# Some split weights start 64 bytes later in their tiles, and the last rotation of each attention unit stands earlier on VectorE

## The chip, the cores and the metric

The kernel runs on one core of one Trainium2 chip. The metric is the device time of one execution in microseconds, as the median of several runs; lower is better. The core's engines are TensorE (PE in the profile; its weight loads are shown apart as PEld), VectorE (DVE), ScalarE (ACT), GpSimd (POOL) and SyncE (SP, which issues most of the DMAs). Each engine works through its own list of instructions in order, and the lists meet at semaphores.

## The reference

The input is 256 tokens of width 1024 in float32. The trunk has two layers, each followed by an MLP with a squared ReLU, and a last RMS norm:

```python
for layer in range(2):
    xn = rms_norm(x, norm_mix[layer])
    if layer % 2 == 0:
        x = x + even_mixer(xn, ...)   # neighbourhood attention and latent attention, 8 heads each
    else:
        x = x + odd_mixer(xn, ...)    # three groups of dilated windows, 16 heads, rope on q and k
    x = x + jnp.square(jax.nn.relu(rms_norm(x, norm_mlp[layer]) @ w1)) @ w2   # 1024 -> 4096 -> 1024
return rms_norm(x, norm_final)
```

In the odd mixer, `hcat = xn @ w_in` gives q, k and v for 3 groups and 16 heads of 64; q and k are rotated by `apply_rope`, and the three groups' outputs are combined by their softmax denominators.

## The kernel before

**Split weights.** All big products are made in pieces of float32 that TensorE takes as `float32r`. Every weight chunk is loaded from HBM as a tile `raw` of 128 partitions x 2048 float32. ScalarE writes `whi`, a rounded copy of it (`split`, L201), and VectorE writes `wlo`, the rest `raw - whi` (L202), each in four pieces of 512 columns. The activations are split in the same way, into the two halves of one tile `pair`: for each of the 8 slices k of the width, 256 tokens of the high part and then 256 of the low part, so that both together are 512 columns that lie side by side. A product is the sum of high x high, high x low and low x high.

**What TensorE streams and what it holds.** A matmul streams one operand (the moving one) past another that a LDWEIGHTS has put into the array (the stationary one, 128 columns here). The next matmul's LDWEIGHTS runs while the current matmul streams. Four kinds of matmul matter here:

- MLP, first product (`up`, in `mlp`): L391 streams 512 columns of `pair` past `whi` of w1, and L394 streams the 256 high columns of `pair` past `wlo`. Per layer there are 16 steps j with 16 of each, 512 of each in all.
- MLP, second product (`down_tokens`, through `mm3`, L205 to L207): 512 columns of `whi` or `wlo` of w2 stream past the hidden activations `hh` or `hl`.
- Odd layer, q and k (`qk_steps`): L911 streams 512 columns of `pair` past `whi` of `w_oqk`, L914 the 256 high columns past `wlo`; 8 of each for each of 48 products (8 units of two heads, three weight chunks, two halves).
- Odd layer, values (`value_steps`, through `mm3`): 512 columns of `whi` or `wlo` of `w_ov` stream past 128 tokens of `pair`; 96 of each of the three products.

**Where the tiles lie.** `whi` and `wlo` come from a pool with three buffers each. In the program as it is allocated, `pair` starts at byte 26944 of each partition, 64 bytes past a multiple of 128. All buffers of `whi` (121216, 129408, 137600), of `wlo`, and of `hh` and `hl` start at multiples of 128, and so does each matmul's slice of them. The slices of `pair` all start 64 bytes past one.

**What sets the order.** PE, ACT and DVE work in the order that a scheduler gives: it goes by the order in which the code issues the steps and by a priority. `tc.high_priority(NORM_PRIO)` lifts the steps under it ahead of others that are issued earlier, above all ahead of the splits of weights that are only needed later. In the odd layer, `ODD_PLAN` says which unit's q and k and which values are made beside which unit's attention. `qk_steps` makes three products for a unit, in the order b = 0, 2, 1: the q of group 0, the k of groups 1 and 2, and the q of groups 1 and 2. After each, `rope` rotates the product: the halves of each head are swapped into `sw` (by DMA for b = 0 and 2, by ScalarE at L931 and L932 for b = 1), VectorE multiplies by the cosines (L934) and by the sines (L935), and adds the two (L937 with a split for b = 0, L944 in two halves into `k12` for b = 2, L940 into `q12` for b = 1). The sum of the two products' halves before it (L920, L922) is under the high priority; `rope` is not. A unit's scores begin with the matmuls at L214, on the q of group 0, and go on at L979, which read `q12` and `k12`.

Of the kernel before, what the change touches and what calls it, by code (L numbers as in the profile page):

```python
# [17 lines left out]
F32R = mybir.dt.float32r  # L18
# [5 lines left out]
P = 128  # L24
# [10 lines left out]
WCH = 2048  # L35
# [3 lines left out]
SPLIT_AHEAD = 2  # L39
WPARTS = 4  # L40
NORM_PRIO = 300

QK_ORDER = (0, 2, 1)

# [24 lines left out]
def trunk(ctx, tc, a, out):  # L69
# [6 lines left out]
    wsp = ctx.enter_context(tc.tile_pool(name="wsp", bufs=WBUFS))  # L76
# [54 lines left out]
    specs = []  # L131

    def plan(name, n):
        for j in range(a[name].shape[0]):
            specs.append((a[name][j], n))

    def plan_mlp(layer):
        for j in (0, 1):
            specs.append((a["w1"][layer, j], WCH))
        for j in range(2, 16):  # L140
            specs.append((a["w1"][layer, j], WCH))
            specs.append((a["w2"][layer, j - 2], WCH))
        for j in (14, 15):
            specs.append((a["w2"][layer, j], WCH))

    CV = 416 + 512
    plan("w_cv", 2 * CV)
# [5 lines left out]
    plan("w_oe", 2 * D)  # L153
    plan_mlp(0)
    for kind, *at in odd_weights():
        specs.append((a[kind][tuple(at)], WCH))
    plan("w_oo", 2 * D)
    plan_mlp(1)

    parts = {}  # L160
    state = {"loaded": 0, "split": 0, "used": 0}

    def load_weight(edges=None, earlier=lambda i: None):
        j = state["loaded"]
        src, n = specs[j]
        raw = wraw.tile([P, WCH], F32, tag="raw", name="raw")
        edges = edges or (0, n)
        for i, c in enumerate(slice(*e) for e in zip(edges, edges[1:])):
            earlier(i)
            nc.sync.dma_start(raw[:, c], src[:, c])  # L170
        parts[j] = [raw, None, None]
        state["loaded"] = j + 1

    def cut(j, i, n):
        w = specs[j][1] // n
        return slice(i * w, (i + 1) * w)

    def split_piece(eng=None):
        j, i = divmod(state["split"], WPARTS)
        if i == 0:  # L180
            parts[j][1:] = (wsp.tile([P, WCH], F32R, tag=n, name=n) for n in ("whi", "wlo"))
        raw, hi, lo = (z[:, cut(j, i, WPARTS)] for z in parts[j])
        state["split"] += 1
        return split(hi, lo, raw, eng)
# [120 lines left out]
    def hand_over(accs, last, n):  # L305

        xT, s = pair_tile(), sum_tile()
        for b in range(4):
            last[b]()
            with tc.high_priority(NORM_PRIO):  # L310
                join(b, accs[b], n, xT)
        return xT, s

    def hand_over_tokens(accs, last, n, scale):
# [4 lines left out]
        def leave(h, t):  # L319
            last(h, t)  # L320
            acc, sc = accs[2 * t + h], column(scale, t)
            with tc.high_priority(NORM_PRIO):
                y = ys[h, t] = scratch([512], "y")
# [3 lines left out]
        def turn(h):  # L327
            with tc.high_priority(NORM_PRIO):
                for b in range(2):
# [187 lines left out]
    def even(ep):  # L517
# [75 lines left out]
        with tc.manual_schedule(engines={ENG.PE, ENG.Activation, ENG.DVE}):  # L593
            def views(j, c0, c1):
                if parts[j][1] is None:
                    parts[j][1:] = (wsp.tile([P, WCH], F32R, tag=n, name=n) for n in ("whi", "wlo"))
                return [z[:, c0:c1] for z in parts[j]]

            for k in range(KT):
                upper, lower = prepare(k, 0, xT)  # L600
                upper()
                if k < 4:
                    c0 = k % 2 * CV
                    wc, wv = views(k // 2, c0, c0 + 416), views(k // 2, c0 + 416, c0 + CV)
                else:
                    wc, wv = views(2, (k - 4) * 416, (k - 3) * 416), None
                if k == 0:

                    nc.vector.tensor_copy(wc[1], wc[0])
                    lower()  # L610
                    nc.vector.tensor_tensor(wc[2], wc[0], wc[1].bitcast(F32), op=ALU.subtract)
                else:
                    lower()
                    split(wc[1], wc[2], wc[0])
                if wv:
                    split(wv[1], wv[2], wv[0])

                if k in (3, 5, 6, 7):
                    squares.pop(0)()
                for w, ps_, n in ((wc, pc, 416), (wv, pv, 512)):  # L620
                    if w is not None:
                        for passes in ((0,), (1,), (2,)) if k == 0 else (range(3),):
                            for t in range(NT):
                                product(ps_[t], n, w, k, t, passes)
            state["split"] = 3 * WPARTS
            for i in range(2 * WPARTS):
                split_piece()
            wv = [z.rearrange("p (k n) -> p k n", k=4) for z in parts[3]]
            for t in range(NT):
                for k in range(4, KT):  # L630
                    product(pv[t], 512, [z[:, k - 4] for z in wv], k, t)
                    if (t, k) == (0, 5):
                        r = rstd(s)
            rs = work.tile([P, 2, NT], F32, tag="rs", name="rs", bufs=1)
            for i, n in enumerate((256, 128)):
                nc.vector.tensor_scalar(rs[:, i, :], r, n ** -0.5, None, ALU.mult)
            dg = [diagonal(r, t) for t in range(NT)]
            turn_c = [c_tail(t, pc[t]) for t in range(NT)]
            state["used"] = 4
            for j in range(4):  # L640
                del parts[j]
            for t in range(NT):
                v_out(t, pv[t])
# [176 lines left out]
        at = -5  # L820
# [11 lines left out]
    def odd(op, xT, s):  # L832
# [22 lines left out]

        def value_steps(b, c, prio=NORM_PRIO, tag="acc"):

# [39 lines left out]
        def qk_steps(d, js=QK_ORDER):  # L897


            hold = {}  # L900

            def gemm(b, f, half):
                if f == 0 and half == 0:
                    hold["w"], hold["q"] = weight(), op.tile([P, 2, T], F32, tag="qk32", name="qk32", bufs=2)
                if half == 0:
                    hold["p"] = bank("acc")
                (wh, wl), pq, q32 = hold["w"], hold["p"], hold["q"]

                cut_of = lambda k: slice((f * KT + k) * P, (f * KT + k + 1) * P)
                for k in (range(0, 6), range(6, KT))[half]:  # L910
                    nc.tensor.matmul(two(pq), wh[:, cut_of(k)], xp[:, k], start=k == 0, stop=False)  # L911
                if half == 1:
                    for k in range(KT):
                        nc.tensor.matmul(pq[:, 0:T], wl[:, cut_of(k)], xh[:, k, :], start=False, stop=k == KT - 1)  # L914
                if half == 1:
                    with tc.high_priority(NORM_PRIO):
                        if f == 0:
                            side = scratch([T], "side")
                            nc.scalar.copy(side, pq[:, T:2 * T])
                            nc.vector.tensor_tensor(q32[:, f], pq[:, 0:T], side, op=ALU.add)  # L920
                        else:
                            nc.vector.tensor_reduce(q32[:, f], pq.rearrange("p (h n) -> p n h", h=2), axis=mybir.AxisListType.X, op=ALU.add)  # L922
                if f == 1 and half == 1:
                    rope(b, q32.rearrange("p f n -> p (f n)"))

            def rope(b, pq):

                sw, r1 = op.tile([P, 512], F32, tag="swap", name="sw", bufs=2), scratch([2, T], "r1")
                change = nc.scalar.copy if b == 1 else nc.sync.dma_start
                for r in range(0, P, 64):  # L930
                    change(sw[r:r + 32], pq[r + 32:r + 64])  # L931
                    change(sw[r + 32:r + 64], pq[r:r + 32])  # L932
                sw = sw.rearrange("p (f n) -> p f n", f=2)
                nc.vector.tensor_tensor(r1, pq.rearrange("p (f n) -> p f n", f=2), cosT.unsqueeze(1).broadcast_to([P, 2, T]), op=ALU.mult)  # L934
                nc.vector.tensor_tensor(sw, sw, sinT.unsqueeze(1).broadcast_to([P, 2, T]), op=ALU.mult)  # L935
                if b == 0:
                    nc.vector.tensor_tensor(r1, r1, sw, op=ALU.add)  # L937
                    split(d["q0h"], d["q0l"], r1)
                elif b == 1:
                    nc.vector.tensor_tensor(d["q12"], r1, sw, op=ALU.add)  # L940
                else:
                    for r in (0, 64):
                        cut = lambda z: z[r:r + 64].rearrange("p j (c n) -> p j c n", n=64)
                        nc.vector.tensor_tensor(d["k12"][r:r + 64, :, :, r:r + 64], cut(r1), cut(sw), op=ALU.add)  # L944

            return [lambda v=(b, f, h): gemm(*v) for b in js for f in range(2) for h in range(2)]
# [223 lines left out]
```

## Time and profile before

| | |
|---|---|
| time, median of 3 runs | 742.25 us (741.9 to 743.02) |
| the profiled execution's own time | 742.68 us |
| its span, from the first to the last instruction | 740.9 us |
| busy: PE, PEld, DVE, ACT, POOL | 732.5, 628.5, 538.6, 471.4, 8.4 us |
| HBM read | 127.16 MB |

The even layer takes the first 113 us of the span or so, the first MLP goes to about 290 us, the odd layer to about 553 us, and the second MLP to the end. The profile's durations of matmuls are modelled at their ends, so a row of it says more by where the next row starts: a row "start us, us, engine line ... xN" of the timeline merges N equal matmuls, and the difference of two rows' starts, divided by the count, is the spacing of the matmuls.

### The profile page before, as it was taken

How to read it: one execution, taken by the hardware profiler on the slowest of the kernel's cores; microseconds unless marked ns; L12 is line 12 of the kernel's file. 1: busy time of each engine (PE TensorE's matmuls, PEld its weight loads, DVE VectorE, ACT ScalarE, POOL GpSimd, SP SyncE). 2: the span in 40 equal slices, each digit the busy share in tenths (PEclk: the TensorE clock that was granted, in tenths of full speed). 3: DMA queues.
4: the chain of work that ended last, by engine and by line, in shares of the span. 5: the costliest groups of instructions: out<-in, count | busy, mean ns of one | idle time of the engine just before them, and what ended most of it. 6: DMA issues, size and time to landing. Idle time of an engine off the chain costs nothing.

```text
span 740.9 us, 11984 instructions
## 1 busy us (share of the span) xinstructions
PE 732.5 (99%) x4539; PEld 628.5 (85%) x4539; DVE 538.6 (73%) x1100; ACT 471.4 (64%) x1020; POOL 8.4 (1%) x20
## 2 busy tenths in 40 slices
PE   9999999999999999999999999999999999999996
PEld 6988998888888887888888888888898888888885
DVE  6878859766665666689968886899559765665674
ACT  7788967554455456468877668687857455455441
POOL 0100000000000001000000000000000000000000
PEclk9999999999999999999999999999999999999999
DMA  8773335565555554655664545455546555545501
GB/s 291 313 263 108 115 114 177 175 218 174 197 197 178 202 188 155 232 160 171 208 220 147 221 145 182 139 192 173 188 152 220 178 175 197 197 171 189 206 4 57
DMA packets 24585, 133.17 MB, mean 180 GB/s; under 512 B 3664, under 2 KB 4816, under 8 KB 10192
## 3 DMA queue, kind: packets, MB, share of 16 engines
q1 hardware_dynamic: 24384, 132.28, 52.0%
q8 instruction: 35, 0.57, 0.3%
q14 instruction: 22, 0.18, 0.1%
q10 hardware_dynamic: 144, 0.13, 0.1%
HBM read 127.16 MB, written 1.05 MB: 173 GB/s over the span
## 4 chain that ended last, share of the span: by engine, by line
PE 94%; DMA 1%; DVE 1%; issue 1%; ACT 1%; SPq 1%; POOLq 0%; POOL 0%
PE w L391 16%; PE acc L205 13%; PE acc L207 13%; PE acc L206 13%; PE acc L911 11%; PE w L394 8%; PE acc L914 5%; PE acc L558 2%; PE w L214 1%; PE w L999 1%; PE w L205 1%; PE w L768 1%; PE w L207 1%; PE w L206 1%; PE w L979 1%
## 5 line engine op out<-in xcount | busy, mean ns | idle before, releaser
L202 DVE TENSOR_TENSOR wlo<-raw,whi 128x512 fp32r<-128x512 f32 (+2 forms) x471 | 303.0, 679 | 68.2 <-ACT whi L201 67.6
L201 ACT CAST whi<-raw 128x512 fp32r<-128x512 f32 (+2 forms) x471 | 261.9, 614 | 140.5 <-PE acc L207 57.0
L391 PE MATMUL w<-pair,whi 128*128 128x512 f32 x512 | 125.0, 395 | 0.0
L391 PEld LDWEIGHTS w<-pair,whi 128*128 128x128 f32 x512 | 95.2, 187 | 22.9 <-DVE pair L242 0.6
L911 PE MATMUL acc<-pair,whi 128*128 128x512 f32 x384 | 101.6, 401 | 0.0
L205 PE MATMUL acc<-whi,hh 128*128 128x512 f32 x250 | 97.9, 392 | 0.0
L207 PE MATMUL acc<-whi,hl 128*128 128x512 f32 x250 | 97.7, 391 | 0.0
L206 PE MATMUL acc<-wlo,hh 128*128 128x512 f32 x250 | 97.6, 390 | 0.0
L911 PEld LDWEIGHTS acc<-pair,whi 128*128 128x128 f32 x384 | 67.7, 188 | 12.4 <-issue 0.2
L398 DVE TENSOR_TENSOR u<-w,side 128x256 f32<-128x256 f32 x64 | 26.9, 421 | 57.2 <-ACT side L397 57.1
L394 PEld LDWEIGHTS w<-pair,wlo 128*128 128x128 f32 x512 | 63.4, 188 | 2.9
L394 PE MATMUL w<-pair,wlo 128*128 128x256 f32 x512 | 63.9, 277 | 0.0
L201 ACT CAST hh<-hsq 128x512 fp32r<-128x512 f32 x32 | 19.9, 622 | 56.4 <-DVE hsq L400 56.4
L207 PEld LDWEIGHTS acc<-whi,hl 128*128 128x128 f32 x250 | 47.0, 188 | 9.7
L914 PEld LDWEIGHTS acc<-pair,wlo 128*128 128x128 f32 x384 | 51.2, 188 | 4.4
L205 PEld LDWEIGHTS acc<-whi,hh 128*128 128x128 f32 x250 | 47.0, 188 | 8.7
L206 PEld LDWEIGHTS acc<-wlo,hh 128*128 128x128 f32 x250 | 46.9, 188 | 8.8
L914 PE MATMUL acc<-pair,wlo 128*128 128x256 f32 x384 | 51.9, 278 | 0.0
L205 PE MATMUL acc<-whi,pair 128*128 128x512 f32 x80 | 32.3, 403 | 0.0
L207 PE MATMUL acc<-whi,pair 128*128 128x512 f32 x80 | 31.5, 393 | 0.0
L206 PE MATMUL acc<-wlo,pair 128*128 128x512 f32 x80 | 31.2, 390 | 0.0
L990 ACT ACTIVATE pp<-sn,dmn 128x384 f32<-128x384 f32 x32 | 19.7, 614 | 9.8 <-DVE dmn L988 8.9
(220 smaller groups left out, 1102.4 us busy)
## 6 DMA issues: line engine op xcount, KB each, us to landing
raw<-in_w SPq DMA_DIRECT2D x64, 1024.0 KB, 4.8
raw<-in_w_oqk SPq DMA_DIRECT2D x24, 1024.0 KB, 4.9
raw<-in_w_ov SPq DMA_DIRECT2D x12, 1024.0 KB, 5.0
raw<-in_w_qk SPq DMA_DIRECT2D x4, 1024.0 KB, 8.6
raw<-in_w_oe SPq DMA_DIRECT2D x4, 1024.0 KB, 5.3
sw<-qk SPq DMA_DIRECT2D x64, 64.0 KB, 2.0
raw<-in_w_oo SPq DMA_DIRECT2D x4, 1024.0 KB, 5.3
bias<-in_rpb SPq DMA_DIRECT2D x8, 256.0 KB, 4.6
```

The costliest lines, as they stand in the source:

```text
L201: a = nc.scalar.copy(hi, src).ins
L202: return a, (eng or nc.vector).tensor_tensor(lo, src, hi.bitcast(F32), op=ALU.subtract).ins
L205: nc.tensor.matmul(o, sh, mh, start=first, stop=False)
L206: nc.tensor.matmul(o, sh, ml, start=False, stop=False)
L207: nc.tensor.matmul(o, sl, mh, start=False, stop=last)
L391: nc.tensor.matmul(two(pu[f]), w[0][:, cut_of(k, f)], xT[2][:, k], start=k == 0, stop=False)
L394: nc.tensor.matmul(pu[f][:, 0:T], w[1][:, cut_of(k, f)], xT[0][:, k, :], start=False, stop=k == KT - 1)
L398: nc.vector.tensor_tensor(u[:, f], pu[f][:, 0:T], side[:, f], op=ALU.add)
L558: nc.tensor.matmul(o[:, 0:n], xs[i], (w[1], w[1], w[2])[i], start=(k, i) == (0, 0), stop=(k, i) == (KT - 1, 2))
L911: nc.tensor.matmul(two(pq), wh[:, cut_of(k)], xp[:, k], start=k == 0, stop=False)
L914: nc.tensor.matmul(pq[:, 0:T], wl[:, cut_of(k)], xh[:, k, :], start=False, stop=k == KT - 1)
L990: nc.scalar.activation(pp, sn, AF.Exp, bias=mn, scale=-1.0, accum_out=z)
```

## The change

There are two edits. Between them they leave the arithmetic as it is.

**The offset.** Every `whi` and `wlo` tile becomes 32 columns (128 bytes) wider, and the 2048 columns used start either at its beginning or 16 columns (64 bytes) later, by a table that goes by the weight:

```diff
+LINE = 16
+SHIFTS = {"w1": (LINE, 0), "w_oqk": (LINE, 0), "w_ov": (LINE, LINE), "w_v": (LINE, LINE)}
...
-            specs.append((a[name][j], n))
+            specs.append((a[name][j], n, SHIFTS.get(name, (0, 0))))
...
+    def split_tiles(j):
+        return [wsp.tile([P, WCH + 2 * LINE], F32R, tag=n, name=n)[:, o:o + WCH] for n, o in zip(("whi", "wlo"), specs[j][2])]
...
-            parts[j][1:] = (wsp.tile([P, WCH], F32R, tag=n, name=n) for n in ("whi", "wlo"))
+            parts[j][1:] = split_tiles(j)
```

For w1 and `w_oqk` only `whi` is moved, for `w_ov` and `w_v` (a chunk of the even layer's values) both parts; w2 and the rest stay. Tiles that are allocated behind these buffers move by 768 bytes, a multiple of 128. The buffers of `whi` now start at 121216, 129536 and 137856. With "0" for a start at a multiple of 128 bytes and "64" for 64 bytes past one, the streamed slice and the slice that the next LDWEIGHTS reads during it are:

| matmuls in PE's order, columns | count | streamed, before and now | loaded beside it, before and now |
|---|---|---|---|
| L391 followed by L391, 512 | 480 | 64, 64 | 0, 64 |
| L391 followed by L394, 512 | 32 | 64, 64 | 0, 0 |
| L394 followed by L394, 256 | 480 | 64, 64 | 0, 0 |
| L911 followed by L911, 512 | 324 | 64, 64 | 0, 64 |
| L911 followed by L914, 512 | 48 | 64, 64 | 0, 0 |
| L914 followed by L911, 256 | 32 | 64, 64 | 0, 64 |
| L914 followed by L914, 256 | 336 | 64, 64 | 0, 0 |
| L205 to L207 on `w_ov`, followed by their like, 512 | 274 | 0, 64 | 64, 64 |
| L205 to L207 on w2, followed by their like, 512 | 717 | 0, 0 | 0, 0 |
| L207 on w2 followed by L391, 512 | 24 | 0, 0 | 0, 64 |

Where something else stands between two of them, such as a transpose, they are in no row of the table.

**The rotation.** The call of `rope` for b = 1, the last of a unit's three, comes under the high priority:

```diff
                 if f == 1 and half == 1:
-                    rope(b, q32.rearrange("p f n -> p (f n)"))
+
+                    with tc.high_priority(NORM_PRIO if b == QK_ORDER[-1] else 0):
+                        rope(b, q32.rearrange("p f n -> p (f n)"))
```

Of the engines' orders only VectorE's changes by this, at four places: the rotations of units 0, 2, 5 and 6. PE, ACT, POOL and SP have the same instructions in the same order as before. Line numbers of the changed kernel are 7 higher than before around `split` and `mlp`, and 9 higher from `rope` on.

Unit 5, on VectorE, before (`q_5092` is the unit's `q12`, `k_1_3256` its `k12`, `r` the product with the cosines, `qk` the sum before the rotation; `qk_5315` belongs to the next unit):

```order
L935 TENSOR_TENSOR sw<-sw,sinT 128x512
L922 TENSOR_REDUCE qk_5240<-acc 128x256
L944 TENSOR_TENSOR k_1_3256<-r_5219,sw 64x8x64 x2
L934 TENSOR_TENSOR r_5292<-qk_5240,cosT 128x512
L202 TENSOR_TENSOR wlo<-raw,whi 128x512 x2
L920 TENSOR_TENSOR qk_5315<-acc,side 128x256
L935 TENSOR_TENSOR sw<-sw,sinT 128x512
L202 TENSOR_TENSOR wlo<-raw,whi 128x512
L940 TENSOR_TENSOR q_5092<-r_5292,sw 128x512
L922 TENSOR_REDUCE qk_5315<-acc 128x256
```

And the same stretch of VectorE now:

```order
L944 TENSOR_TENSOR sw<-sw,sinT 128x512
L929 TENSOR_REDUCE qk_5240<-acc 128x256
L953 TENSOR_TENSOR k_1_3256<-r_5219,sw 64x8x64
L943 TENSOR_TENSOR r_5292<-qk_5240,cosT 128x512
L953 TENSOR_TENSOR k_1_3256<-r_5219,sw 64x8x64
L209 TENSOR_TENSOR wlo<-raw,whi 128x512 x2
L944 TENSOR_TENSOR sw<-sw,sinT 128x512
L927 TENSOR_TENSOR qk_5315<-acc,side 128x256
L949 TENSOR_TENSOR q_5092<-r_5292,sw 128x512
L209 TENSOR_TENSOR wlo<-raw,whi 128x512
```

The addition into `q12` moves ahead of one split of a weight piece, which now stands right behind it; the second half of `k12` trades places with the product by the cosines, and both halves still stand ahead of `q12`.

Unit 0, on VectorE, before (`q_3260` is its `q12`, `k_0_3254` its `k12`):

```order
L935 TENSOR_TENSOR sw<-sw,sinT 128x512
L934 TENSOR_TENSOR r_3623<-qk_3583,cosT 128x512
L944 TENSOR_TENSOR k_0_3254<-r_3562,sw 64x8x64 x2
L920 TENSOR_TENSOR qk_3646<-acc,side 128x256
L935 TENSOR_TENSOR sw<-sw,sinT 128x512
L202 TENSOR_TENSOR wlo<-raw,whi 128x512
L940 TENSOR_TENSOR q_3260<-r_3623,sw 128x512
L922 TENSOR_REDUCE qk_3646<-acc 128x256
```

And now:

```order
L943 TENSOR_TENSOR r_3623<-qk_3583,cosT 128x512
L944 TENSOR_TENSOR sw<-sw,sinT 128x512
L209 TENSOR_TENSOR wlo<-raw,whi 128x512
L953 TENSOR_TENSOR k_0_3254<-r_3562,sw 64x8x64
L944 TENSOR_TENSOR sw<-sw,sinT 128x512
L927 TENSOR_TENSOR qk_3646<-acc,side 128x256
L949 TENSOR_TENSOR q_3260<-r_3623,sw 128x512
L953 TENSOR_TENSOR k_0_3254<-r_3562,sw 64x8x64
```

Here the split moves ahead of `k12`, and half of `k12` now stands behind `q12`; L979 reads both, so what it needs is complete after the same number of VectorE instructions as before.

More of the change, by code (lines that the diff above doesn't have):

```diff
@@ L134, in plan @@
         for j in range(a[name].shape[0]):
-            specs.append((a[name][j], n))
+            specs.append((a[name][j], n, SHIFTS.get(name, (0, 0))))
     def plan_mlp(layer):
         for j in (0, 1):
-            specs.append((a["w1"][layer, j], WCH))
+            specs.append((a["w1"][layer, j], WCH, SHIFTS["w1"]))
         for j in range(2, 16):
-            specs.append((a["w1"][layer, j], WCH))
-            specs.append((a["w2"][layer, j - 2], WCH))
+            specs.append((a["w1"][layer, j], WCH, SHIFTS["w1"]))
+            specs.append((a["w2"][layer, j - 2], WCH, (0, 0)))
         for j in (14, 15):
-            specs.append((a["w2"][layer, j], WCH))
+            specs.append((a["w2"][layer, j], WCH, (0, 0)))
     CV = 416 + 512
@@ L155, in trunk @@
     for kind, *at in odd_weights():
-        specs.append((a[kind][tuple(at)], WCH))
+        specs.append((a[kind][tuple(at)], WCH, SHIFTS[kind]))
     plan("w_oo", 2 * D)
@@ L164, in load_weight @@
         j = state["loaded"]
-        src, n = specs[j]
+        src, n, _ = specs[j]
         raw = wraw.tile([P, WCH], F32, tag="raw", name="raw")
@@ L595, in views @@
                 if parts[j][1] is None:
-                    parts[j][1:] = (wsp.tile([P, WCH], F32R, tag=n, name=n) for n in ("whi", "wlo"))
+                    parts[j][1:] = split_tiles(j)
                 return [z[:, c0:c1] for z in parts[j]]
```

## The prediction

> **What bounds the kernel now.** I read the page's busy times first, then the chain that ended last, then TensorE's waits.
>
> ```profile
> span 740.9 us, 11984 instructions
> PE 732.5 (99%) x4539; PEld 628.5 (85%) x4539; DVE 538.6 (73%) x1100; ACT 471.4 (64%) x1020; POOL 8.4 (1%) x20
> PE 94%; DMA 1%; DVE 1%; issue 1%; ACT 1%; SPq 1%; POOLq 0%; POOL 0%
> ```
>
> ```profile
> PE acc L117 <- DVE warm L112: 1.2, 1, 1.2
> PE w L979 <- DVE q L940: 0.7, 1, 0.7
> PE acc L205 <- DVE obl L202: 0.2, 1, 0.2
> ```
>
> The second fence is all that PE waited for: 1.2 us at the start, and inside the program 0.7 and 0.2 us. So two things alone can shorten the kernel: that L979 doesn't wait, worth 0.7 us, or that matmuls follow each other more closely. The groups by form say which matmuls there are:
>
> ```profile
> L391 PE MATMUL w<-pair,whi 128*128 128x512 f32 x512 | 125.0, 395 | 0.0
> L911 PE MATMUL acc<-pair,whi 128*128 128x512 f32 x384 | 101.6, 401 | 0.0
> L206 PE MATMUL acc<-wlo,hh 128*128 128x512 f32 x250 | 97.6, 390 | 0.0
> L394 PE MATMUL w<-pair,wlo 128*128 128x256 f32 x512 | 63.9, 277 | 0.0
> ```
>
> Their busy times overlap, so the spacing is read from the starts in the timeline. One step of the first MLP, L391 and L394, then the second product's L205 to L207:
>
> ```profile
> 158.51 3.89 PE L391 MATMUL w<-pair,whi 128*128 128x512 f32 x16
> 162.25 1.99 PE L394 MATMUL w<-pair,wlo 128*128 128x256 f32 x16
> 164.07 0.39 PE L205 MATMUL acc<-whi,hh 128*128 128x512 f32 x1
> ...
> 165.22 0.39 PE L207 MATMUL acc<-whi,hl 128*128 128x512 f32 x1
> ...
> 169.53 0.39 PE L391 MATMUL w<-pair,whi 128*128 128x512 f32 x1
> ```
>
> 16 L391 take 162.25 - 158.51 = 3.74 us, 233.8 ns each. Between 165.22 and 169.53 stand 19 matmuls of w2, 226.8 ns each. Both kinds stream 512 columns past 128, and neither waits. They differ in where the operands lie: for L391 the streamed slice starts 64 bytes past a multiple of 128 and the loaded one at a multiple (I write 64/0); for w2 both start at multiples (0/0). The 16 L394, 64/0 with 256 columns, take 113.8 ns each. Three more spacings, of the odd layer's q and k (L911, 64/0), of its values (0/64), and of the last products of the kernel (256 columns, 0/0):
>
> ```profile
> 400.37 2.02 PE L911 MATMUL acc<-pair,whi 128*128 128x512 f32 x8
> 402.23 1.07 PE L914 MATMUL acc<-pair,wlo 128*128 128x256 f32 x8
> ```
>
> ```profile
> 295.00 0.39 PE L205 MATMUL acc<-whi,pair 128*128 128x512 f32 x1
> ...
> 302.78 0.39 PE L206 MATMUL w<-wlo,pair 128*128 128x512 f32 x1
> ```
>
> ```profile
> 730.21 0.28 PE L205 MATMUL w<-whi,hh 128*128 128x256 f32 x1
> ...
> 734.40 0.28 PE L207 MATMUL w<-whi,hl 128*128 128x256 f32 x1
> ```
>
> L911: 1.86 us for 8, 232.5 ns each. Values: 34 spacings in 7.78 us, 228.8 ns. The last ones: 35 spacings in 4.19 us, 119.7 ns. With 512 columns equal halves are the closest (226.8, against 228.8 and 233.8); with 256 columns it is the other way about, 119.7 with equal halves and 113.8 with unequal ones.
>
> **The offset, part by part.** It brings the 512-column matmuls on w1, `w_oqk` and `w_ov` to 64/64, which no row of before shows with this kind of weight load. The bounds are 226.8 ns, if what counts is that both operands lie in equal halves, and 235.5 ns, if each operand past its multiple costs by itself (the streamed one 233.8 - 226.8 = 7.0, the loaded one 228.8 - 226.8 = 2.0). I take 226.8: the 256-column rows exclude a plain price for the streamed operand's place, since there 64/0 is the closer one, by 5.9 ns.
>
> - w1: 480 pairs L391-L391 x (233.8 - 226.8) = 3.4 us. The 32 pairs that lead to L394 stay 64/0, and so do L394's own, which are at their closer spacing already.
> - `w_oqk`: a block of eight L911 takes 1.86 us; then 7 x 226.8 + 233.8 (the last, before L914, stays 64/0) = 1.82 us, 0.04 less, x 48 blocks = 1.9 us. Against it, 32 L914 that stand before an L911 become 64/64: 32 x 5.9 = 0.2 us. Net 1.7 us.
> - `w_ov`: 274 pairs x 2.0 = 0.5 us.
> - `w_v`: 24 matmuls by the same 2 ns, under 0.1 us; the 24 L207 before an L391 become 0/64, 24 x 2.0 = 0.05 us the other way. Together nothing.
>
> The sum is 5.6 us. All of it lies on the path, since PE is busy without a gap there. What must keep up is hidden work with room:
>
> ```profile
> L202 DVE TENSOR_TENSOR wlo<-raw,whi 128x512 fp32r<-128x512 f32 x456 | 295.5, 684 | 66.6 <-ACT whi L201 66.0
> L202 DVE TENSOR_TENSOR hl<-hsq,hh 128x512 fp32r<-128x512 f32 x32 | 22.1, 691 | 2.4
> L922 DVE TENSOR_REDUCE qk<-acc 128x256 f32<-128x512 f32 x24 | 16.5, 687 | 8.7 <-PE acc L914 8.5
> 290.00:553.00 263.00, 262.18 (x1830) 227.33 (x1829) 210.65 (x426) 193.34 (x407) 2.60 (x3) 1.00 0.54 180
> ```
>
> The second row reads a tile at 64 and one at 0, and takes 691 ns where the first, all at 0, takes 684: 7 ns is my bound for what the moved `whi` costs VectorE, on an engine that is idle for 52 us of the odd layer's 263 (the last row, of the busy times by stretch: PE, PEld, DVE, ACT, POOL, the clock, the DMA share). There it waits for PE (third row), so it starts sooner when PE comes sooner. If that cover were gone, PE would wait at L979 or at the transposes, and up to the odd layer's share, 2.2 us, would be given back.
>
> The Trainium skill, SBUF — State Buffer, section "SBUF: two separate sides", says that on the engines' side only the port that VectorE and GpSimd share is contended and that PE never waits for anyone; and, also of the Trainium skill, TensorE: Matmul & The Clock Gate, section "Step-by-step: what each phase is for", gives TensorE two independent read ports, for the streamed operand and for the weights. By these the offset's 5.6 us would be nothing. The trace disagrees as far as it goes: equal shapes, none waiting, at 226.8 and 233.8 ns.
>
> **The rotation, step by step.** The 0.7 us are in unit 5:
>
> ```profile
> 472.12 0.69 DVE L935 TENSOR_TENSOR sw<-sw,sinT 128x512 f32<-128x512 f32 x1 [1.39 <-DMA sw<-qk]
> ...
> 476.87 0.68 DVE L935 TENSOR_TENSOR sw<-sw,sinT 128x512 f32<-128x512 f32 x1
> 477.46 0.68 DVE L202 TENSOR_TENSOR wlo<-raw,whi 128x512 fp32r<-128x512 f32 x1
> 478.07 0.68 DVE L940 TENSOR_TENSOR q<-r,sw 128x512 f32<-128x512 f32 x1
> ```
>
> ```profile
> 477.86 0.28 PE L214 MATMUL w<-q0h,q0l 64*128 64x256 f32 x2
> ...
> 478.81 1.09 PE L979 MATMUL w<-k,q 128*64 128x128 f32 x16 [0.66 <-DVE q L940]
> ```
>
> The split at 477.46 stands ahead of L940, and now behind it: L940 starts 0.61 us sooner and L979 with it, at about 478.2 instead of 478.81. Since PE also arrives here a little sooner (three blocks of eight L911 stand between 472 and 477, 0.1 us), I count 0.5 us. VectorE's chain from 472.12 on has no gap, so nothing else of it moves; the split that is put off is one of many made ahead. In the other three units PE didn't wait for L940, and nothing is won. The swaps for b = 1 are ScalarE's, whose order stays, and no DMA is moved.
>
> **Sum.** 5.6 + 0.5 = 6.1 us off the profiled execution's own 742.68 us (its span of 740.9 and 1.8 around it) is 736.6; this execution lay 0.4 above the median, so off 742.25: 736.2 us.
>
> **The rivals.**
>
> - *Both places cost by themselves.* Then 64/64 is 235.5 ns: L391 480 x 1.7 = 0.8, L911 324 x 2 = 0.6, `w_ov` 274 x 6.7 = 1.8, 3.2 us in all, less 0.5 for the rotation: 742.25 + 2.7 = 745.0. For it speaks that 64/0 and 0/64 are the same distance apart and cost 7.0 and 2.0 ns, so it isn't the distance alone; and these rows, where L911 at 64 stands before a transpose whose weights lie at 64:
>
> ```profile
> 426.60 1.55 PE L911 MATMUL acc<-pair,whi 128*128 128x512 f32 x6
> 427.99 0.27 PE L999 MATMUL w<-ident,pp 128*128 128x128 f32 x1
> ```
>
> 1.39 us for six is 231.7 ns, no closer; but only one of the six is 64/64, and before another kind of load. Against it speak the 256-column rows. It decides if L391's spacing comes out above 233.8. Chance 0.06.
> - *The place doesn't matter to TensorE*, and the 7 ns come from elsewhere, such as the kind of output or the order of the loads. Only the rotation is left: 741.75. The two spacings that reverse between 512 and 256 columns speak against it. Chance 0.07. The two rules of the Trainium skill named above would give this time.
> - *What counts is the place within 256 bytes.* The wider tiles put every other buffer 128 bytes off, so that only a third of the pairs would be equal: 5.6 / 3 + 0.5 = 2.4 us, 739.9; w2's own pairs would be unequal in two of three too, at a price between 0 and 7.0 ns x 717 x 2/3 = 3.3 us, so up to 743.2. No row of before tells 128 from 256, since all these buffers lie 8192 bytes apart. Chance 0.08, half of it above 740.8.
> - *The gain is partly given back* by waits in the odd layer, as costed above: 736.2 + 2.2 = 738.4. Chance 0.09.
>
> **How the numbers follow.** My forecast, 736.2, has 0.70. Its own range is 734.8 to 737.6: a spacing read over 19 matmuls is good to 0.5 ns, 0.5 us over some 1100 pairs, and the runs of before lay 1.1 us apart. The range that should hold the time 8 times in 10 reaches over the waits given back and to the case of 256 bytes: 734.2 to 740.0. A difference of 0.2%, 1.5 us, is about what a measurement of this kernel can tell from no change: faster means below 740.8, slower above 743.7. Faster: 0.70 for the forecast, 0.09 for the gain partly given back and 0.04 for half of the 256 bytes, 0.83. Same: 0.07 and the other 0.04, 0.11. Slower: 0.06.
>
> **What would show it right or wrong.** In the changed profile, 16 L391 in 3.64 us instead of 3.74 and blocks of eight L911 in 1.82 show the offset's terms; w2's matmuls should stay at 226.8 and L394's at 113.8. L979 should no longer be among PE's waits with more than 0.2 us. L391 at 233 with w2 unchanged refutes equal halves; L391 that differs from step to step by buffer, in turns of three, shows the 256 bytes; new PE waits in the odd layer show the gain given back. A time above 740.8 makes the prediction wrong.

## The result, and the profile after

The changed kernel takes 746.4 us (median of 6 runs, 746.02 to 746.67) against 742.28 us of the kernel before beside it: a ratio of 1.0054, 95% interval 1.0041 to 1.0067. It is slower by 4 us, where 6 us less had been forecast.

The page of the changed kernel, its span and busy times, and then all that TensorE waits for (in each row: what it waited with and the line, the releaser, us in total, times, longest):

```profile
span 744.5 us, 11981 instructions
...
PE 736.5 (99%) x4539; PEld 631.6 (85%) x4539; DVE 540.1 (73%) x1100; ACT 471.4 (63%) x1020; POOL 8.4 (1%) x20
```

```profile
PE acc L121 <- DVE warm L116: 1.2, 1, 1.2
PE acc L565 <- ACT whi L208: 0.5, 1, 0.5
PE acc L212 <- DVE obl L209: 0.2, 1, 0.2
```

The span is 3.6 us longer (740.9 before) and PE's busy time 4.0 us longer, with the same 4539 matmuls. No wait explains it: the 0.7 us at L979 (now L988) are gone, and one of 0.5 us has come at the start of the program. So the matmuls themselves follow each other less closely. Three groups of before that the prediction did not quote:

```profile
L205 PE MATMUL acc<-whi,hh 128*128 128x512 f32 x250 | 97.9, 392 | 0.0
L207 PE MATMUL acc<-whi,hl 128*128 128x512 f32 x250 | 97.7, 391 | 0.0
L914 PE MATMUL acc<-pair,wlo 128*128 128x256 f32 x384 | 51.9, 278 | 0.0
```

And the groups of the changed kernel (L398 was L391, L918 was L911, L212 to L214 were L205 to L207, L401 was L394, L921 was L914):

```profile
L398 PE MATMUL w<-pair,whi 128*128 128x512 f32 x512 | 124.1, 394 | 0.0
L918 PE MATMUL acc<-pair,whi 128*128 128x512 f32 x384 | 101.1, 400 | 0.0
L212 PE MATMUL acc<-whi,hh 128*128 128x512 f32 x250 | 99.1, 397 | 0.0
L214 PE MATMUL acc<-whi,hl 128*128 128x512 f32 x250 | 98.3, 393 | 0.0
L213 PE MATMUL acc<-wlo,hh 128*128 128x512 f32 x250 | 98.2, 393 | 0.0
L401 PE MATMUL w<-pair,wlo 128*128 128x256 f32 x512 | 65.4, 280 | 0.0
L921 PE MATMUL acc<-pair,wlo 128*128 128x256 f32 x384 | 52.8, 280 | 0.0
```

The two groups that the change was to shorten did get shorter, by 0.9 and 0.5 us. The groups that were to stay grew: w2's three by 1.2, 0.6 and 0.6 us, L401 by 1.5, L921 by 0.9. Since the rows overlap, I also summed the distances from each matmul's start to the next one's, group by group, over the whole trace. The differences to before are, in us:

| | after | forecast |
|---|---|---|
| L398, streams `pair`, loads `whi` of w1 | -0.95 | -3.4 |
| L918, the same in the odd layer | -0.54 | -1.9 |
| values of the odd layer, 512 columns | +0.38 | -0.5 |
| w2, three lines | +2.74 | 0 |
| L401, 256 columns past `wlo` of w1 | +1.49 | 0 |
| L921, the same in the odd layer | +0.97 | +0.2 |
| L221, with the wait before L988 | -0.74 | -0.5 |
| all others, above all the first 14 us with the new wait | +0.33 | 0 |
| sum | +3.68 | -6.1 |

The sum is the longer span to within 0.1 us. Two steps of the first MLP in the timeline of the changed kernel show the manner of it:

```profile
147.90 3.80 PE L398 MATMUL w<-pair,whi 128*128 128x512 f32 x16
151.54 2.05 PE L401 MATMUL w<-pair,wlo 128*128 128x256 f32 x16
153.43 0.39 PE L212 MATMUL acc<-whi,hh 128*128 128x512 f32 x1
...
159.03 3.88 PE L398 MATMUL w<-pair,whi 128*128 128x512 f32 x16
162.74 2.04 PE L401 MATMUL w<-pair,wlo 128*128 128x256 f32 x16
164.62 0.39 PE L212 MATMUL acc<-whi,hh 128*128 128x512 f32 x1
...
170.12 1.56 PE L398 MATMUL w<-pair,whi 128*128 128x512 f32 x6
```

The first step's 16 L398 take 3.64 us (227.5 ns each, the forecast's spacing), the second's 3.71 (231.9). L401 takes 1.89 and 1.88 us for 16 (118 ns, where the prediction's step had 113.8). The 24 matmuls of w2 take 5.60 us (233.3 ns) and 5.50 (229.2), before 226.8 each. The steps after these repeat that in turns of three, as the buffers of `whi` do.

### The profile page after: what moved, and what is told of

The parts are those of the page before. It is cut to its first block, busy times and chain, and to the rows that moved or that the text cites. A ratio compares the mean times of both kernels' runs of the same rounds, so it can differ in the third digit from the quotient of the medians.

```text
span 744.5 us, 11981 instructions
## 1 busy us (share of the span) xinstructions
PE 736.5 (99%) x4539; PEld 631.6 (85%) x4539; DVE 540.1 (73%) x1100; ACT 471.4 (63%) x1020; POOL 8.4 (1%) x20
## 4 chain that ended last, share of the span: by engine, by line
PE 96%; issue 1%; ACT 1%; DMA 1%; SPq 0%; DVE 0%; POOLq 0%; POOL 0%
PE w L398 16%; PE acc L212 13%; PE acc L213 13%; PE acc L214 13%; PE acc L918 12%; PE w L401 8%; PE acc L921 6%; PE acc L565 2%; PE w L221 1%; PE w L1008 1%; PE w L212 1%; PE w L214 1%; PE w L213 1%; PE w L775 1%; PE w L988 1%
## 5 line engine op out<-in xcount | busy, mean ns | idle before, releaser
L398 PE MATMUL w<-pair,whi 128*128 128x512 f32 x512 | 124.1, 394 | 0.0
L398 PEld LDWEIGHTS w<-pair,whi 128*128 128x128 f32 x512 | 95.4, 188 | 22.2 <-DVE pair L249 0.8
L918 PE MATMUL acc<-pair,whi 128*128 128x512 f32 x384 | 101.1, 400 | 0.0
L212 PE MATMUL acc<-whi,hh 128*128 128x512 f32 x250 | 99.1, 397 | 0.0
L214 PE MATMUL acc<-whi,hl 128*128 128x512 f32 x250 | 98.3, 393 | 0.0
L918 PEld LDWEIGHTS acc<-pair,whi 128*128 128x128 f32 x384 | 67.8, 188 | 12.2 <-issue 0.2
L405 DVE TENSOR_TENSOR u<-w,side 128x256 f32<-128x256 f32 x64 | 26.9, 420 | 56.3 <-ACT side L404 56.0
L401 PEld LDWEIGHTS w<-pair,wlo 128*128 128x128 f32 x512 | 64.7, 188 | 2.7
L401 PE MATMUL w<-pair,wlo 128*128 128x256 f32 x512 | 65.4, 280 | 0.0
L214 PEld LDWEIGHTS acc<-whi,hl 128*128 128x128 f32 x250 | 46.9, 188 | 11.1
L921 PEld LDWEIGHTS acc<-pair,wlo 128*128 128x128 f32 x384 | 51.9, 188 | 4.1
L212 PEld LDWEIGHTS acc<-whi,hh 128*128 128x128 f32 x250 | 47.0, 188 | 9.4
L921 PE MATMUL acc<-pair,wlo 128*128 128x256 f32 x384 | 52.8, 280 | 0.0
L212 PE MATMUL acc<-whi,pair 128*128 128x512 f32 x80 | 32.4, 405 | 0.0
L214 PE MATMUL acc<-whi,pair 128*128 128x512 f32 x80 | 31.4, 392 | 0.0
L997 DVE CUSTOM_DVE_ANT_0 sn<-w,mask 128x384 f32<-128x384 f32 x32 | 17.5, 546 | 11.1 <-PE w L988 11.1
```

The costliest lines, as they stand in the source:

```text
L212: nc.tensor.matmul(o, sh, mh, start=first, stop=False)
L214: nc.tensor.matmul(o, sl, mh, start=False, stop=last)
L398: nc.tensor.matmul(two(pu[f]), w[0][:, cut_of(k, f)], xT[2][:, k], start=k == 0, stop=False)
L401: nc.tensor.matmul(pu[f][:, 0:T], w[1][:, cut_of(k, f)], xT[0][:, k, :], start=False, stop=k == KT - 1)
L405: nc.vector.tensor_tensor(u[:, f], pu[f][:, 0:T], side[:, f], op=ALU.add)
L997: nc.vector.tensor_tensor_reduce(out=sn, in0=ss[j][:, 0:384], in1=mask[:, i, :], op0=ALU.add, op1=ALU.min, scale=-(HD ** -0.5), scalar=3e3 ...
```

## The experiments

All kernels are the one before with the two tables made free: columns added to the tiles of (`whi`, `wlo`), and the column at which each part of a weight starts (16 columns are 64 bytes).

```diff
+PADS = (0, 0)
+SHIFTS = {}
...
+        return [wsp.tile([P, WCH + p], F32R, tag=n, name=n)[:, o:o + WCH] for n, p, o in zip(("whi", "wlo"), PADS, specs[j][2])]
```

To read them, take the distance d from the start of the streamed slice to the start of the slice that the next LDWEIGHTS reads, within 256 bytes of a partition. It follows from the addresses that the program gives to the tiles. Before, d is 64 for L391 and L394, 0 for w2, and 192 for the values of the odd layer. In the changed kernel the buffers of `whi` lie 8320 bytes apart instead of 8192, so that neighbours differ by 128 in it: for L398 d is 0 with the middle one of the three and 128 with the other two, for L401 it is 64 or 192, and for w2 0 or 128, the two in turns within each step, since the buffers of `wlo` differ too.

### The two edits apart, and the width apart from the offset

**The rotation alone** (e1):

```diff
+                    with tc.high_priority(NORM_PRIO if b == QK_ORDER[-1] else 0):
+                        rope(b, q32.rearrange("p f n -> p (f n)"))
```

> The rotation alone, tiles as before. My prediction counted 0.5 us for it: 741.7 us, L979 no longer among PE's waits with more than 0.2 us, matmul spacings as before (L391 233.8, w2 226.8, L394 113.8 ns). If the rotation is a cost, so that it explains the slower result, this run comes out above 744 us.

Measured: 742.13 us, ratio 1.0 (0.999 to 1.0009). Its timeline in unit 5:

```profile
477.46 0.68 DVE L946 TENSOR_TENSOR q<-r,sw 128x512 f32<-128x512 f32 x1
...
478.22 0.98 PE L985 MATMUL w<-k,q 128*64 128x128 f32 x14
```

The addition into `q12` starts 0.61 us sooner than before, L985 (L979 before) starts at 478.22 instead of 478.81, and no wait stands in its row. This is the step as forecast. Its 0.7 us are 0.1% of the kernel, which the interval neither shows nor excludes.

**The wider tiles alone** (e2), with nothing moved inside them:

```diff
+PADS = (32, 32)
+SHIFTS = {}
```

> Tiles of whi and wlo 128 bytes wider, every offset 0, no rotation. Theory A (the place within 256 bytes counts, and the wider tiles put every other buffer 128 bytes off): w2's matmuls go from 226.8 to some 231 ns and L394 from 113.8 to some 117.5 ns as in the changed kernel, 717 x 4 ns + 816 x 3 ns = 5 us, so about 747 us. Theory B (each operand's place past 128 bytes costs by itself): places within 128 bytes are those of before, so 742.3 us and spacings as before.

Measured: 746.23 us, 1.0056 (1.0043 to 1.0068): the whole loss, without any offset. One step of it:

```profile
148.32 3.84 PE L396 MATMUL w<-pair,whi 128*128 128x512 f32 x16
152.00 1.99 PE L399 MATMUL w<-pair,wlo 128*128 128x256 f32 x16
153.82 0.39 PE L210 MATMUL acc<-whi,hh 128*128 128x512 f32 x1
...
159.41 3.89 PE L396 MATMUL w<-pair,whi 128*128 128x512 f32 x16
```

The 24 matmuls of w2 take 5.59 us here (232.9 ns). In all, w2 is 2.79 us longer than before, L399 1.01 and L919 0.86. The 128 bytes more between the buffers do this, and w2 is not among the weights that the table moves. On the other side, L396 is 0.74 us and L916 0.42 us shorter here too: in one step of three, such as the first one shown, d is 192 for them, and 16 L396 take 3.68 us there (230 ns) or 3.66 (229). So most of what these groups gained in the changed kernel, 0.95 and 0.54 us, comes with the width and not with the offset.

**Width of 256 bytes, three offsets** (e3, e4, e5). The tiles of `whi` are 64 columns wider, so that all buffers keep their place within 256 bytes; `wlo` stays as it was.

```diff
+PADS = (64, 0)
-SHIFTS = {}
+SHIFTS = {'w1': (48, 0), 'w_oqk': (48, 0), 'w_ov': (48, 0)}
```

That is e3, with 192 bytes and d = 0 for L396. In e4, 16 stands for 48 (64 bytes as in the change, d = 128); in e5 the table stays empty (d = 64 as before).

> whi tiles 256 bytes wider, wlo as before, whi of w1, w_oqk and w_ov 192 bytes in, no rotation: streamed pair and loaded whi are then equal within 256 bytes in all three buffers, and w2's operands too. Theory A: L391 and L911 at 226.8 ns, w2 at 226.8 and L394 at 113.8 as before, 742.3 - 3.4 - 1.7 - 0.2 = 737.0 us. Theory B: 64 past 128 on both sides as in the changed kernel, 235.5 ns for L391, so 744 us or more.

> As the kernel with 192 bytes, but 64 bytes in: pair and whi are then 128 bytes apart within 256 in all three buffers, w2's operands equal. Theory A: L391 about 232.5 ns in every step as in two of three buffers of the changed kernel, w2 and L394 as before, so 742.3 - 480 x 1.3 ns = 741.7 us and clearly above the kernel with 192 bytes. Theory B, which knows only 128 bytes: the same as the kernel with 192 bytes.

> whi tiles 256 bytes wider, every offset 0, no rotation: the control for the width. Places within 256 bytes are those of before in every buffer, so theory A expects 742.3 us, w2 at 226.8 ns, L391 at 233.3 and L394 at 113.7 ns. If any widening or moving of buffers costs, it comes near the 746.2 us of the 128 bytes.

Measured: 742.31 us (1.0001, 0.9992 to 1.0009), 742.29 (1.0001, 0.9992 to 1.0009) and 741.96 (0.9998, 0.9989 to 1.0007). The same step in e3, e4 and e5:

```profile
147.36 3.80 PE L396 MATMUL w<-pair,whi 128*128 128x512 f32 x16
151.00 2.05 PE L399 MATMUL w<-pair,wlo 128*128 128x256 f32 x16
152.88 0.39 PE L210 MATMUL acc<-whi,hh 128*128 128x512 f32 x1
...
158.36 3.80 PE L396 MATMUL w<-pair,whi 128*128 128x512 f32 x16
```

```profile
148.25 3.88 PE L396 MATMUL w<-pair,whi 128*128 128x512 f32 x16
151.97 1.98 PE L399 MATMUL w<-pair,wlo 128*128 128x256 f32 x16
153.79 0.39 PE L210 MATMUL acc<-whi,hh 128*128 128x512 f32 x1
...
159.24 3.88 PE L396 MATMUL w<-pair,whi 128*128 128x512 f32 x16
```

```profile
148.31 3.89 PE L396 MATMUL w<-pair,whi 128*128 128x512 f32 x16
152.04 1.99 PE L399 MATMUL w<-pair,wlo 128*128 128x256 f32 x16
153.87 0.39 PE L210 MATMUL acc<-whi,hh 128*128 128x512 f32 x1
```

L396 takes 3.64 us with d = 0 (227.5 ns), 3.72 with d = 128 (232.5) and 3.73 with d = 64 (233.1). Modulo 128, e3 and e4 are the same: both operands 64 bytes past a multiple. So equality within 256 bytes counts, and equality within 128 bytes does not. The width by itself costs nothing when it is a multiple of 256 (e5, and w2 in all three within 0.7 us of before).

But e3 is no faster than before, although L396 gains 2.75 us and L916 0.80. Its L399 takes 1.88 us for 16 (117.5 ns) and in all 1.58 us more than before, L919 0.77 more, w2 0.63, the values of the odd layer 0.73. And `wlo`, which L399 loads, has not been moved in e3. This is what the next runs are for.

### Why the 256-column matmuls give the gain back

In before, e3 and e4 alike, `wlo` lies at d = 64, and L394 runs at 113.4 or at 117.8 ns, for a whole stream of 16 the same. What goes with it is the last spacing of the 512-column stream ahead of it. In before, all 27 MLP steps in which that was 233 ns or more go on at 113.4, and all 5 with 231 or less at 117.8. In e4, whose places differ from e3's in `whi` alone, 30 steps with 233 or more go on at 113.4, and 2 with 229 at 117.8. In e3 that spacing is 225 or 226 in 31 of 32 steps, and all 31 go on at 117.8; the last, with 230, goes on at 113.4.

**The last 512-column matmul in two** of 256 (e6, otherwise e3), so that another spacing leads in:

```diff
+                        for v, c in ([(xT[0][:, k], slice(0, T)), (xT[1][:, k], slice(T, 2 * T))] if (f, k) == (1, 7) else [(xT[2][:, k], None)]):
```

> As the kernel with whi 192 bytes in (there L391 came to 226.8 ns, but L394 went from 113.7 to 117.8 ns with its places unchanged), and the last 512-column matmul ahead of each 256-column stream (L391 with f = 1, k = 7; L911 with k = 7) is made as two of 256 columns. Theory C (at the same places the 256-column stream has two steady rhythms, 113.7 and 117.8, and the end of the stream before decides which): the entry is another one, L394 and L914 may fall to 113.7 ns, 480 x 4.1 + 336 x 2.5 ns = 2.8 us less, about 739.8 us. Theory D (the places of the operands decide): L394 stays at 117.8 and the time at 742.3 us or a little more.

Measured: 743.03 us, 1.0013 (1.0004 to 1.0022). The two halves take about 113 and 119 ns, and the stream stays at 117.8. So a short spacing ahead of it is not what leads into the closer rhythm.

**`wlo` at the three other places** (e7, e8, e9: 64, 128 and 192 bytes in; `whi` at d = 0 in all, `w_ov` 192 bytes in with both parts). To make room, the tile `warm`, on which TensorE works at the very start, is halved, and twice as many matmuls go over it.

```diff
-    warm = const.tile([P, 512], mybir.dt.bfloat16, name="warm")
+    warm = const.tile([P, 256], mybir.dt.bfloat16, name="warm")
...
-            nc.tensor.matmul(idle, warm[:, 0:P], warm, start=True, stop=True)
+            nc.tensor.matmul(idle[:, 0:256], warm[:, 0:P], warm, start=True, stop=True)
...
-    keep_warm(7)
+    keep_warm(14)
...
+PADS = (64, 64)
+SHIFTS = {'w1': (48, 16), 'w_oqk': (48, 16), 'w_ov': (48, 48)}
```

> whi and wlo both 256 bytes wider, whi of w1, w_oqk and both parts of w_ov 192 bytes in (equal with pair within 256), wlo of w1 and w_oqk 64 in, so 128 from pair; the warm-up tile halved to make room, its 7 matmuls of 512 columns now 14 of 256. L391, w2 at 226.8 ns; theory D: L394 settles at some one value by its place; theory C: at 113.7 or 117.8 by the entry.

> The same with wlo of w1 and w_oqk 128 in, so 64 past pair on the other side than before. Theory D by distance alone (64 either way is equal): L394 at 113.7 ns, 739.5 us or less; theory C: either of 113.7 and 117.8.

> The same with wlo 192 in, so equal with pair within 256 bytes as the kernel's last products are with their weights, which took 119.7 ns. Theory D: L394 at 119.7 ns, 816 x 2 ns = 1.6 us more than with whi alone moved, 744 us. Theory C: 113.7 or 117.8.

Measured: 743.47 us (1.0017, 1.0008 to 1.0026), 741.73 (0.9991, 0.9982 to 1.0) and 743.1 (1.0013, 1.0004 to 1.0022). One stream of L399 and the start of what follows, in e7, e8 and e9:

```profile
161.46 2.08 PE L399 MATMUL w<-pair,wlo 128*128 128x256 f32 x16
163.38 0.39 PE L210 MATMUL acc<-whi,hh 128*128 128x512 f32 x1
```

```profile
162.50 2.05 PE L399 MATMUL w<-pair,wlo 128*128 128x256 f32 x16
164.38 0.39 PE L210 MATMUL acc<-whi,hh 128*128 128x512 f32 x1
```

```profile
162.89 2.07 PE L399 MATMUL w<-pair,wlo 128*128 128x256 f32 x16
164.80 0.39 PE L210 MATMUL acc<-whi,hh 128*128 128x512 f32 x1
```

That is 1.92, 1.88 and 1.91 us for 16. These runs also differ from e3 in the values of the odd layer. In e3 only `whi` of `w_ov` is moved, so that d is 0 and 192 in turns; in e7 to e9 both parts are moved, and d is 0 throughout. 34 spacings of the values, from the first row to the second, in e3 and in e7:

```profile
294.77 0.40 PE L210 MATMUL acc<-whi,pair 128*128 128x512 f32 x1
...
302.66 0.39 PE L211 MATMUL w<-wlo,pair 128*128 128x512 f32 x1
```

```profile
294.50 0.39 PE L210 MATMUL acc<-whi,pair 128*128 128x512 f32 x1
...
302.22 0.39 PE L211 MATMUL w<-wlo,pair 128*128 128x512 f32 x1
```

They take 7.89 us (232.1 ns) and 7.72 (227.1), against 228.8 ns before with d = 192 throughout. In all the values are 0.3 us shorter than before in e7, e8 and e9, and 0.7 us longer in e3: equal places help where the whole stream has them.

From start to start, the steady spacings of matmuls of one kind are, over all these runs:

| d, loaded slice after streamed one | 0 | 64 | 128 | 192 |
|---|---|---|---|---|
| 512 columns, L391 | 226.7 (e3) | 233.3 (before, e5) | 232.6 (e4) | 229 (e2, one step of three) |
| 256 columns, L394 | 120.0 (e9) | 113.4 or 117.8 | 120.3 (e7) | 117.8 (e8) |

So no place of all of `wlo` brings 113.4 behind a last spacing of 225 to 227 ns. At d = 64 both rhythms occur; at d = 192 a single one of e8's 32 MLP streams, behind a spacing of 231 ns, ran at 113.4. What is needed at d = 64 is another way in.

**The first 256-column matmul in two** (e10: 128 and 128 columns; e12: 64 and 192; otherwise e3, with all places as there):

```diff
+CUTS = [slice(0, 128), slice(128, 256)]
...
+                    for c in (CUTS if (f, k) == (0, 0) else [slice(0, T)]):
+                        nc.tensor.matmul(pu[f][:, c], w[1][:, cut_of(k, f)], xT[0][:, k, c], start=False, stop=k == KT - 1)
```

> As the kernel with whi 192 bytes in, and the first 256-column matmul of each L394 and L914 stream made as two of 128 columns. Theory C (the rhythm of a 256-column stream is decided by how it is entered; in the kernel before, last spacings of L391 of 233 ns and more were followed by 113.7, of 231 and less by 117.8): the entry changes while all places stay; if it falls on the other side, L394 goes to 113.7 and the time to 739 to 740 us; if not, it stays at 117.8 and the time is 742.3 + 0.3. Theory D (places decide): 117.8 in any case.

> As the kernel with the first 256-column matmul made as two of 128, but of 64 and 192 columns: another entry. Theory C: 113.7 or 117.8 by where it falls, and if the halves left it at 117.8, this one may not. Theory D: 117.8.

Measured: 748.96 us (1.0087, 1.0073 to 1.0101) for e10 and 748.94 (1.0085, 1.0071 to 1.0099) for e12. The end of one stream in e10:

```profile
151.73 1.41 PE L401 MATMUL w<-pair,wlo 128*128 128x256 f32 x11
152.98 0.39 PE L211 MATMUL acc<-whi,hh 128*128 128x512 f32 x1
```

The last 11 matmuls take 1.25 us, 113.6 ns each: at e3's places, and behind e3's L396, the stream now runs in the closer rhythm, as do 31 of e10's 32 MLP streams and all of e12's. So the way in decides, not the place alone. But the way there is dear: the first spacings are 58, 114, 166, 119, 120, 119, 118 ns, where e3 has 118 for each matmul. The stream becomes longer than e3's (151.03 to 152.98 in the step shown, 1.95 us against 1.88), and so does that of the odd layer, which has 8 such matmuls and not 16 to win it back: against before, e10 spends 3.68 us more in the MLPs' group of 256 columns and 5.75 in the odd layer's, where e3 spends 1.58 and 0.77.

**The first 128 columns of `wlo` laid 64 bytes off** (e11). `wlo` is at d = 64, except the slice that is loaded first, which lies at d = 128 and is written by a VectorE instruction of its own. Then the last L402 spacing is that of d = 128, about 233 ns, and all others stay at d = 0. The tiles and the warm-up are as in e7.

```diff
+SHIFTS = {'w1': (48, 64), 'w_oqk': (48, 64), 'w_ov': (48, 48)}
...
+        return [t[:, o:o + WCH] for t, o in zip(z, specs[j][2])] + ([z[1][:, 16:16 + P]] if specs[j][2] == (48, 64) else [])
...
+            for o, c in ((parts[j][3], slice(0, P)), (lo[:, P:], slice(P, 512))):
+                nc.vector.tensor_tensor(o, raw[:, c], hi[:, c].bitcast(F32), op=ALU.subtract)
...
+                    nc.tensor.matmul(pu[f][:, 0:T], w[2] if (f, k) == (0, 0) else w[1][:, cut_of(k, f)], xT[0][:, k, :], start=False, stop=k == KT - 1)
```

> As the kernel with whi 192 bytes in, both tiles 256 bytes wider, and only the first slice of 128 columns of wlo of w1 and w_oqk laid 64 bytes off, 128 from pair within 256, all others 64 from it as before; the split writes that slice by an instruction of its own; warm-up tile halved. The last L391 is then followed by 232 to 233 ns as in the kernel with wlo 64 in. Theory C: L394 then runs at 113.7 ns in all steps with L391 at 226.8, about 742.3 - 3.0 - 0.5 = 738.5 us (one of two L914 streams as well). Theory D: L394 at 117.8, 742 us.

Measured: 739.04 us (738.91 to 739.55), 0.9953 (0.994 to 0.9965). It is faster than both kernels, by some 3.4 us than before. Its groups, and a step:

```profile
L402 PE MATMUL w<-pair,whi 128*128 128x512 f32 x512 | 122.4, 391 | 0.1
...
L405 PE MATMUL w<-pair,wlo 128*128 128x256 f32 x512 | 63.9, 277 | 0.0
```

```profile
147.66 3.81 PE L402 MATMUL w<-pair,whi 128*128 128x512 f32 x16
151.31 2.00 PE L405 MATMUL w<-pair,wlo 128*128 128x256 f32 x16
153.14 0.39 PE L216 MATMUL acc<-whi,hh 128*128 128x512 f32 x1
```

16 L402 take 3.65 us and 16 L405 1.83: both streams are short at once, as in no other run. The last L402 spacing is 232 or 233 ns in all 32 MLP steps, and all 32 go on at 113.4. Against before, L402 wins 2.58 us, its counterpart in the odd layer 0.69 and the values 0.26; L405 stays as it was, and the 256 columns of the odd layer lose 0.47.

## Why the prediction was wrong

**What bounds the kernel** was right. In every run PE's waits behind the warm-up come to 1.6 us at most (e4), and the differences between the runs lie in the spacing of its matmuls.

**The step that failed** is the premise of the offset's term: 226.8 ns, "if what counts is that both operands lie in equal halves", and then "I take 226.8". Two operands in equal halves of 128 bytes (64/64) cost 232.5 ns in e4 and 227.5 in e3. What counts is the place within 256 bytes. No row of before tells the two apart, since all its buffers of one kind lie the same way in both; the prediction said so itself, in the rival *What counts is the place within 256 bytes*, and gave it a chance of 0.08. This rival is what happened: its sign in the trace, L391 differing from step to step in turns of three, is in the timeline above. The reading against the distance, that 64/0 and 0/64 "are the same distance apart and cost 7.0 and 2.0 ns", holds within 128 bytes only: within 256 bytes L391 is at 64 and the values are at 192, and at 192 L396 takes 229 ns as well (e2).

**Term by term.** w1's 3.4 us became 0.95 and `w_oqk`'s 1.9 became 0.54, together 1.5, of which e2 has 0.74 and 0.42 without any offset; a third of the whole, 5.6 / 3 = 1.9, had been the rival's figure with the values in it. The values' 0.5 us turned into a loss of 0.38; where their d is 0 throughout (e7 to e9, e11) they win 0.3. w2's own loss, 2.74 us, lies inside the rival's bound of 0 to 3.3.

**What the rival left out too** is L394 and L914, said to stay "at their closer spacing already". They cost 2.5 us, and with them the time went past the rival's 743.2. Their 113.8 ns is one of two rhythms at an unchanged place, and in before it comes only behind a last 512-column spacing of 233 ns or more. By shortening that spacing the change takes it away (e3); by the 128 bytes it also moves `wlo` to d = 192 in two steps of three, where 117.8 was all that e8's MLP steps showed but one. With all of `wlo` in one place the gain on the 512 columns and the loss on the 256 columns go together: even at the right offset (e3) the forecast 6 us would have been none. Laying one slice aside (e11) takes them apart, and then 3.4 us are won, not 6.

**The conclusion from 256 columns** ("the 256-column rows exclude a plain price") held: the rival *Both places cost by themselves* would have given 235.5 ns at e3's 64/64, and it is 227.5. **The rotation** was right in its mechanism (e1). Its 0.7 us, of which 0.5 had been counted, are in the trace but too small to be timed. The gain given back by waits in the odd layer did not come: VectorE and ScalarE cause no new wait there.

The prediction cited the Trainium skill, TensorE: Matmul & The Clock Gate, section "Step-by-step: what each phase is for", for two read ports that do not disturb each other, and SBUF — State Buffer, section "SBUF: two separate sides", by which PE waits for no one. The runs speak against both as far as they mean that places are free: e3 and e4 differ in nothing but 128 bytes of `whi`'s offset, and their L396 by 5 ns in 227.5.

**What stays open.** That equality within 256 bytes closes the spacing is shown; by what part of the chip it does so isn't. Nor is it shown why a last spacing of 233 ns leads into 113.4 and not into 117.8, whether the spacing itself or something that goes with it does this (e11 also moves the slice that is loaded first), or why the values in e3, with d of 0 and 192 in turns, are slower than with either alone. In the odd layer the entry rule is looser: in before all 6 streams of 256 columns behind 231 ns or less are in the slower rhythm and all 42 behind 233 or more in the closer one; in e3 all 31 behind 229 or less are in the slower one, but also 3 of the 17 behind 231 or more.

## What to carry to other kernels

Before moving an operand, work out the addresses of all that shares its pool: a tile that grows by anything but a multiple of the size that matters (256 bytes here) moves the other buffers off their places too, and here the weights that nobody meant to touch cost more than the moved ones won. Where the matmuls bind and nothing waits, read the spacing of several steps, not of one, since the spacing of a stream depends on the stream ahead of it. And test a premise on two kernels that differ in it alone: e3 and e4 settle at once what the prediction argued from four rows.

## What the runs showed of the hardware

- A 512-column matmul past 128 columns follows its like in 226.7 ns if the streamed and the next loaded slice start at equal places within 256 bytes of a partition, in 232 to 234 ns at 64 or 128 bytes off, and in 229 ns at 192 (e2; the values of before). It takes a whole stream of equal places: with 0 and 192 in turns the values took 232 ns (e3), with 0 throughout 227 (e7). With 256 columns equal places are among the worst, 120.0 ns, as is 128 bytes off, 120.3; 113.4 is reached at 64 bytes off, and at 192 by one MLP stream of 32 (e8).
- A stream has a memory: at one set of places 256-column matmuls keep 113.4 or 117.8 ns to their end, by the way they were entered (e3 against e10 and e12).
- A stream needs some matmuls to settle: L396 in e3 goes 229, 233, 230, 227 ns and then stays at 226 or 227, and w2 behind L399 takes about ten, with spacings from 224 to 236, until it is there.
